# Softmax sums kept and divided out behind attention: forgetting heads on y^T, differential heads in the norm

## The chip, the core and the metric

The kernel runs on one core of one Trainium2 chip. The metric is the device time of one execution in microseconds, and lower is better. Everything is float32 at the level of the reference; TensorE works on pairs of a high and a low part.

## The reference

One decoder block on x of 1024 positions by 1024 channels. Two attention branches run side by side, each is gated, projected and merged.

```python
h = rms_norm(x, g_pre[l], NORM_EPS)
proj = jnp.einsum('bsd,dn->bsn', h, w_in[l])
qa, ka, va, fa, za, qb, kb, vb, zb, gates = jnp.split(proj, SPLIT_POINTS, axis=-1)
# forgetting heads (8 of 64 channels): softmax over causal logits plus sums of log_f
p = jax.nn.softmax(logits, axis=-1)
ya = merge_heads(p @ va) * jax.nn.silu(za)
# differential heads (4, q and k in two halves of 64, v of 128)
p = jax.nn.softmax(logits, axis=-1)
pd = p[:, :, 0] - lam * p[:, :, 1]
yb = rms_norm(pd @ vb, g_subln[l], SUBLN_EPS) * (1.0 - lam_init)
yb = merge_heads(yb) * jax.nn.silu(zb)
gate_a, gate_b = jnp.split(jax.nn.sigmoid(gates), N_BRANCHES, axis=-1)
merged = gate_a * (ya @ w_branch[l, 0]) + gate_b * (yb @ w_branch[l, 1])
x = x + rms_norm(merged @ w_out[l], g_post[l], NORM_EPS)
```

A softmax row is the exponentials divided by their sum. That sum is one number for each head and position, so it can be divided out before or after the product with v. The norm over the 128 channels of a differential head doesn't change under a factor for a position, but for its small constant.

## The kernel before

A product of two float32 matrices is made of three products of high and low parts. The high part is a cast on ScalarE, the low part the difference on VectorE or GpSimd. The order of the instructions on each engine is laid down when the kernel is built, by a scheduler that places them along a timeline of its own; buffers rotate in pools.

The stages, with their times in the profiled execution: the norm, x^T and the projections of v (0 to 113 us); attention (113 to 598); sums of x^T halves for Winograd products and the first, plain gate pass (598 to 650); seven paired gate passes d=1 to 7 (650 to 773); branch products (775 to 863); the output product and the last norm.

Attention has eight units. Units 0 to 3 are differential heads (t = 0 to 3), units 4 to 7 pairs of forgetting heads (t = 4 to 7). A unit works through groups of two blocks of 128 query positions. For each block, `s_row` (L380 to L401) makes the logits on TensorE, VectorE adds the mask or bias and takes the row's minimum (L393; the sign is turned), ScalarE takes the exponential with the row's sum in `le` (L398), and VectorE its reciprocal (L400). A forgetting head's row is scaled by it on GpSimd (L512). In a differential head the second sum's reciprocal is multiplied by minus lambda (L481), the second half scaled by that on GpSimd (L482), the first half scaled by its own on ScalarE (L484), and the two are added on GpSimd (L485). `av` (L403 to L453) turns the blocks on TensorE (L420), splits them on ScalarE and VectorE (L423, L424) and multiplies by v (L444), which gives y^T, channels by positions. y^T is stored in DRAM (`y_d`). Between groups stand, as filling for TensorE, the q and k projections of the next unit, the projections of z (stored in `z_d`), and for differential heads `sum_squares` and `subln_scales` (L357 to L361), which makes the norm's factor of each position, 4 KB a head, stored in `rs_d`. The function `rstd_of` (L108 to L110) is two GpSimd operations.

In a paired gate pass, `gates_pair` loads two weight blocks raw_0 and raw_1 (L789, from a pool with two buffers of that kind). `left_operands` makes the seven left sides of a Winograd product: raw blocks or their sums S_g (L646, GpSimd), each cast by ScalarE (L633) with the low part on VectorE, or GpSimd for raw blocks m=2 and m=4 (L634). `wino` multiplies (L682), ScalarE copies the first result (L685) and VectorE adds the others (L675) into c_g and cu_g; these get a sigmoid (L744) and are stored in `g_d` (L745). Next to that, `y_work(t, c)` (L731 to L741) finishes half of one y^T, 128x512: it loads z (L734), for t under 4 also the norm's factor over all partitions (L737) and multiplies by it (L738, VectorE), then y times z (L739, GpSimd), the sigmoid of z (L740, ScalarE) and y times that (L741, VectorE). The names yd and yf are the differential and the forgetting heads' y^T, zs and rb the loaded tiles. The forgetting heads' parts come in d=5 (t=4), d=6 (t=5) and d=7 (t=6 and 7). The tiles c_g, cu_g, zs and rb share eight buffers. Then y^T is split (L824, L825), and the branch products (L835) begin with the forgetting heads; their weights are cast on ScalarE (hi_br, L229), the low part on VectorE or GpSimd (lo_br, L233).

## Time and profile before

| what | us |
|---|---|
| median of 3 runs (lowest and highest) | 963.38 (962.74 to 963.75) |
| profiled execution, its own time | 964.18 |
| its span | 962.4 |
| TensorE busy in the span | 900.5 |
| VectorE busy | 635.3 |
| GpSimd busy | 489.6 |
| ScalarE busy | 435.9 |

A profile is one execution, taken by the hardware profiler; times are microseconds from the start of the span, unless marked ns. Engines: PE is TensorE's matmul, PEld its load of weights, DVE VectorE, ACT ScalarE, POOL GpSimd, SP the engine that issues the DMAs; a name with q behind is an engine's sequencer. PEclk is the clock granted to TensorE, 1.00 is full speed. "A <- B" in the waits means that A stood idle until B was done. The chain is the work that ended last, followed back from the last instruction to what released it. L12 is line 12 of the kernel, out<-in names the tiles.

### The profile page before, as it was taken

Reading aid. Unit: us, or ns where it says so; the run is one execution under the profiler, and the core shown is the slowest. Engines: PE = TensorE matmul, PEld = TensorE weight load, DVE = VectorE, ACT = ScalarE, POOL = GpSimd, SP = SyncE. Lnnn points to the kernel's source line nnn. Section 1 sums busy time; section 2 is a strip of 40 time slices with the busy share of each in tenths; the row PEclk is TensorE's granted clock in tenths of the full one; section 3 lists DMA queues with packets and bytes.
Section 4 is the critical chain, followed back from the end, with each engine's and each line's share of the span. In section 5 each row is a group of like instructions: output and inputs, shape, how many; then the busy total and the mean of one; then the engine's idle time right before and its main releaser. Section 6 shows DMA issues by size and latency. Waiting matters only on the chain.

```text
span 962.4 us, 13682 instructions
## 1 busy us (share of the span) xinstructions
PE 900.5 (94%) x4600; PEld 752.0 (78%) x4600; DVE 635.3 (66%) x1180; ACT 435.9 (45%) x862; POOL 489.6 (51%) x460
## 2 busy tenths in 40 slices
PE   7999989999999999999999998879999989999992
PEld 5999867777887888888888886658887768887871
DVE  7731258978768765656566477985667683559875
ACT  3421125665656674555555566243444361324331
POOL 7100035446545464344533554935566735878972
PEclk9999989999999999999999999989999999999997
DMA  9532444424334341524225231254444697210144
GB/s 315 190 110 93 144 128 112 107 77 120 97 96 137 99 144 43 150 67 130 81 88 146 85 88 56 78 179 149 143 153 134 191 357 247 67 44 1 46 151 153
DMA packets 109896, 120.17 MB, mean 125 GB/s; under 512 B 9969, under 2 KB 79601, under 8 KB 109826
## 3 DMA queue, kind: packets, MB, share of 16 engines
q1 hardware_dynamic: 109826, 119.30, 40.0%
q8 instruction: 36, 0.59, 0.3%
q14 instruction: 34, 0.28, 0.1%
HBM read 77.26 MB, written 29.43 MB: 111 GB/s over the span
## 4 chain that ended last, share of the span: by engine, by line
PE 45%; DVE 17%; POOL 13%; issue 10%; DMA 7%; ACT 6%; SPq 2%; DVEq 0%; POOLq 0%; ACTq 0%
PE pb L835 9%; PE pv L192 9%; PE pz L243 7%; PE pq L243 5%; PE pk L243 4%; POOL S_g L646 3%; PE ypf L444 3%; PE ptf L420 2%; DMA raw<-in_w_in_dram 2%; DMA swk<-rawk 2%; SPq L284 2%; DVE Pd L393 1%; POOL a_g L634 1%; PE ypd L444 1%; PE Sf L391 1%
## 5 line engine op out<-in xcount | busy, mean ns | idle before, releaser
L192 PE MATMUL pv<-wvhi,hT 128*128 128x264 f32 (+2 forms) x384 | 88.8, 323 | 0.4 <-DVE hT L178 0.4
L682 PE MATMUL x_g<-T,a_g 128*128 128x512 f32 x336 | 82.1, 399 | 6.3 <-DVE a_g L634 2.5
L243 PE MATMUL pk<-hT,hi_k 128*128 128x512 f32 x256 | 84.5, 402 | 1.7 <-ACT rawk L280 1.7
L243 PE MATMUL pz<-hT,hi_z 128*128 128x512 f32 x256 | 84.2, 399 | 0.1
L243 PE MATMUL pq<-hT,hi_q 128*128 128x512 f32 x256 | 83.4, 399 | 0.0
L682 PEld LDWEIGHTS x_g<-T,a_g 128*128 128x128 f32 x336 | 63.4, 191 | 23.5 <-DVE a_g L634 4.0
L835 PE MATMUL pb<-yT,hi_br 128*128 128x512 f32 x256 | 78.9, 390 | 1.9 <-ACT hi_br L229 1.6
L682 PE MATMUL x_o<-wo_op,a_o 128*128 128x512 f32 x336 | 77.4, 391 | 2.3 <-ACT a_o L633 1.2
L682 PEld LDWEIGHTS x_o<-wo_op,a_o 128*128 128x128 f32 x336 | 62.8, 188 | 16.9 <-ACT a_o L633 2.1
L192 PEld LDWEIGHTS pv<-wvhi,hT 128*128 128x128 f32 x384 | 64.3, 189 | 6.1 <-DVE hT L178 0.7
L682 PE MATMUL x_g<-hT,a_g 128*128 128x512 f32 x252 | 62.2, 400 | 6.1 <-DVE a_g L634 5.4
L398 ACT ACTIVATE Pd<-Pd,mxd 128x128 f32<-128x128 f32 (+7 forms) x64 | 49.5, 773 | 29.9 <-DVE mxd L393 28.1
L512 POOL TENSOR_SCALAR Pf<-Pf,lf 128x1024 f32<-128x1024 f32 (+3 forms) x64 | 47.9, 752 | 29.0 <-DVE lf L400 27.2
L424 DVE TENSOR_TENSOR plf<-ptf,phf 128x512 fp32r<-128x512 f32 (+1 forms) x80 | 50.0, 635 | 18.8 <-ACT phf L423 17.8
L192 PE MATMUL pv<-wvlo,hT 128*128 128x512 f32 (+2 forms) x192 | 61.8, 324 | 0.6 <-DVE wvlo L148 0.6
L682 PEld LDWEIGHTS x_g<-hT,a_g 128*128 128x128 f32 x252 | 48.4, 193 | 17.6 <-DVE a_g L634 5.8
L482 POOL TENSOR_SCALAR Pd<-Pd,ld 128x128 f32<-128x128 f32 (+7 forms) x32 | 25.5, 798 | 71.1 <-DVE ld L481 38.2
L508 POOL TENSOR_TENSOR cb<-cb,trim 128x128 f32<-128x128 f32 x64 | 29.5, 464 | 63.3 <-DVE mxf L393 46.7
L398 ACT ACTIVATE Pf<-Pf,mxf 128x1024 f32<-128x1024 f32 (+3 forms) x64 | 49.7, 778 | 21.4 <-DVE mxf L393 20.8
L835 PEld LDWEIGHTS pb<-yT,hi_br 128*128 128x128 f32 x256 | 47.8, 188 | 12.7 <-ACT hi_br L229 2.0
L243 PEld LDWEIGHTS pk<-hT,hi_k 128*128 128x128 f32 x256 | 48.0, 192 | 11.2 <-issue 2.1
L243 PEld LDWEIGHTS pq<-hT,hi_q 128*128 128x128 f32 x256 | 48.0, 191 | 9.1
(243 smaller groups left out, 2440.5 us busy)
## 6 DMA issues: line engine op xcount, KB each, us to landing
raw<-in_w_in_dram SPq DMA_DIRECT2D x14, 512.0 KB, 4.0
g_d<-c_g SPq DMA_DIRECT2D x21, 256.0 KB, 2.0
vb_d<-vbs SPq DMA_DIRECT2D x8, 512.0 KB, 5.9
va_d<-vas SPq DMA_DIRECT2D x8, 512.0 KB, 3.0
raw_k<-in_w_in_dram SPq DMA_DIRECT2D x8, 512.0 KB, 4.3
raw_q<-in_w_in_dram SPq DMA_DIRECT2D x8, 512.0 KB, 4.4
V<-vb_d SPq DMA_DIRECT2D x4, 1024.0 KB, 7.4
raw_z<-in_w_in_dram SPq DMA_DIRECT2D x8, 512.0 KB, 5.4
```

The source lines that it names most:

```text
L192: nc.tensor.matmul(ps[n], lhsT=hT[hp][k // 4][i // 4][:, k % 4, hs], rhs=wt[k][:, a:b], start=first, stop=(k == KT - 1 and hp == 1))
L243: nc.tensor.matmul(ps, lhsT=a[:, k, :], rhs=hT[h][k // 4][c][:, k % 4, :], start=(k == 0 and a is hi and h == 0), stop=(k == KT - 1 and a ...
L284: nc.sync.dma_start(sw[b * 32:(b + 1) * 32, :], raw[o * 32:(o + 1) * 32, :])
L398: nc.scalar.activation(pr[:, 0:n], pr[:, 0:n], AF.Exp, bias=mx[:, len(pcs) - 1:len(pcs)], scale=-1.0, accum_out=le)
L424: nc.vector.tensor_tensor(pl[:, 0:n], pt[:, 0:n], ph[:, 0:n], op=ALU.subtract)
L444: nc.tensor.matmul(o, lhsT=a, rhs=b[:, src], start=(j == 0 and n == 0), stop=(odd == 1 and jj == g and n == len(prods) - 1))
L482: nc.gpsimd.tensor_scalar(p2[:, 0:n], p2[:, 0:n], l2, 1.0, op0=ALU.mult, op1=ALU.mult)
L508: nc.gpsimd.tensor_tensor(diag, diag, trim, op=ALU.add)
L512: nc.gpsimd.tensor_scalar(p1[:, 0:n], p1[:, 0:n], l1, 1.0, op0=ALU.mult, op1=ALU.mult)
L646: eng.tensor_tensor(comb[name], x, y, op=op)
L682: nc.tensor.matmul(x[m], lhsT=a[:, ai, k, :], rhs=right[m][bi][k], start=(k == 0 and n == 0), stop=(k == 3 and n == 2))
L835: nc.tensor.matmul(ps, lhsT=a[:, kk, :], rhs=yT[g][h][:, k % 2, sl], start=(k == 0 and a is hi and h == 0), stop=(k == 3 and a is lo))
```

## The change

The sums are kept in a tile `lsum` (12 heads, 128 positions by 8 blocks), where the exponential writes them.

For forgetting heads the exponentials go into the product with v as they are. After a unit, VectorE takes the reciprocals of 128x8 a head, and `save_sums` stores them in `l_d` in DRAM, by position, one DMA a head. `y_work` loads them over 64 partitions for each of the two heads (into rb, two DMAs) and multiplies y^T by rb on VectorE, ahead of the multiplication by z.

For differential heads the first half stays unscaled, and the second is scaled by minus lambda times the first sum over the second. So y^T is larger by the first sum. The norm takes that away, if its constant is multiplied by the square of the sum: `subln_scales` loads the saved sums, GpSimd squares them, and VectorE adds them to the sum of squares.

The diff's core:

```diff
@@ -92,6 +92,9 @@
     onesr = const.tile([P, 32], F32R, name="onesr")
     nc.gpsimd.tensor_scalar(onesr, ident[:, 0:32], 0.0, 1.0, op0=ALU.mult, op1=ALU.add)
     sub_rs = const.tile([P, 4, 8], F32, name="sub_rs")
+    sub_l = const.tile([P, 4, 8], F32, name="sub_l")
+    lsum = const.tile([P, 12, 8], F32, name="lsum")
+    linv = const.tile([P, 8, 8], F32, name="linv")
 
     hT = [[[hpool.tile([P, 4, CH], F32R, tag=f"h{part}{kh}{sh}", name=f"hT{part}{kh}{sh}")
             for sh in range(2)] for kh in range(2)] for part in range(2)]
@@ -102,6 +105,7 @@
     y_d = [dram.tile([P, S], F32, name=f"y_d{t}") for t in range(8)]
     g_d = [[dram.tile([P, S], F32, name=f"g_d{d}_{b}") for b in range(2)] for d in range(KT)]
     ss_d = dram.tile([4, S], F32, name="ss_d")
+    l_d = dram.tile([12, S], F32, name="l_d")
     rs_d = dram.tile([4, S], F32, name="rs_d")
     z_d = [dram.tile([P, S], F32, name=f"z_d{t}") for t in range(8)]
 
@@ -355,9 +359,12 @@
             nc.sync.dma_start(ss_d[t:t + 1, sl], sq[0:1])
 
         def subln_scales(t):
-            rs = sub_rs[:, t]
+            rs, ls = sub_rs[:, t], sub_l[:, t]
             nc.sync.dma_start(rs, ss_d[t].rearrange("(p j) -> p j", j=8))
-            rstd_of(rs, rs, P, SUB_EPS)
+            nc.sync.dma_start(ls, l_d[8 + t].rearrange("(p j) -> p j", j=8))
+            nc.gpsimd.tensor_tensor(ls, ls, ls, op=ALU.mult)
+            nc.vector.scalar_tensor_tensor(rs, ls, P * SUB_EPS, rs, op0=ALU.mult, op1=ALU.add)
+            rstd_of(rs, rs, P, 0.0)
             nc.sync.dma_start(rs_d[t].rearrange("(p j) -> p j", j=8), rs)
 
         def pieces(i):
@@ -377,7 +384,11 @@
                 nc.sync.dma_start(f32(t[a]), f32(src[b, qs]))
             return t
 
-        def s_row(T, m, i, X, bias, boff, nm):
+        def save_sums(h, src):
+
+            nc.sync.dma_start(l_d[h].rearrange("(i p) -> p i", p=P), src)
+
+        def s_row(T, m, i, X, bias, boff, nm, le):
 
             A, B = (T["TA"], T["KA"]) if m == 0 else (T["TB"], T["KB"])
             n = (i + 1) * P
@@ -394,11 +405,9 @@
                     out=pr[:, a:b], in0=ps, in1=bias[:, boff + a:boff + b], scale=-0.125,
                     scalar=BIG if j == 0 else mx[:, j - 1:j], op0=ALU.add, op1=ALU.min,
                     accum_out=mx[:, j:j + 1])
-            le = small.tile([P, 1], F32, tag="l", name=f"l{nm}_{m}_{i}", bufs=8)
             nc.scalar.activation(pr[:, 0:n], pr[:, 0:n], AF.Exp,
                                  bias=mx[:, len(pcs) - 1:len(pcs)], scale=-1.0, accum_out=le)
-            nc.vector.reciprocal(le, le)
-            return pr, le
+            return pr
 
         def av(rows, g, vt, hoff, fox, evac, nm, final):
 
@@ -475,13 +484,17 @@
                     boff = S - (i + 1) * P
                     if "X" not in rows:
                         rows["X"] = [swapped(T, m, i // 2, f"d{u}") for m in range(2)]
-                    p1, l1 = s_row(T, 0, i, rows["X"][0], dmask, boff, f"d{u}")
-                    p2, l2 = s_row(T, 1, i, rows["X"][1], dmask, boff, f"d{u}")
+
+                    l1 = lsum[:, 8 + u, i:i + 1]
+                    l2 = small.tile([P, 1], F32, tag="l", name=f"l{u}_{i}", bufs=8)
+                    p1 = s_row(T, 0, i, rows["X"][0], dmask, boff, f"d{u}", l1)
+                    p2 = s_row(T, 1, i, rows["X"][1], dmask, boff, f"d{u}", l2)
                     n = (i + 1) * P
-                    nc.vector.tensor_tensor(l2, l2, nlam, op=ALU.mult)
+                    nc.vector.reciprocal(l2, l2)
+                    nc.vector.tensor_scalar(
+                        l2, l2, l1, nlam, op0=ALU.mult, op1=ALU.mult)
                     nc.gpsimd.tensor_scalar(
                         p2[:, 0:n], p2[:, 0:n], l2, 1.0, op0=ALU.mult, op1=ALU.mult)
-                    nc.scalar.activation(p1[:, 0:n], p1[:, 0:n], AF.Copy, scale=l1)
                     nc.gpsimd.tensor_tensor(
                         p1[:, 0:n], p1[:, 0:n], p2[:, 0:n], op=ALU.add)
                     rows[i] = p1
@@ -508,10 +521,8 @@
                     nc.gpsimd.tensor_tensor(diag, diag, trim, op=ALU.add)
                     if "X" not in rows:
                         rows["X"] = swapped(T, m, i // 2, f"f{u}")
-                    p1, l1 = s_row(T, m, i, rows["X"], cb[m], 0, f"f{u}")
-                    nc.gpsimd.tensor_scalar(
-                        p1[:, 0:n], p1[:, 0:n], l1, 1.0, op0=ALU.mult, op1=ALU.mult)
-                    rows[i] = p1
+                    h = 2 * t + m
+                    rows[i] = s_row(T, m, i, rows["X"], cb[m], 0, f"f{u}", lsum[:, h, i:i + 1])
 
                 def evac(m, g):
                     def run(yp):
@@ -611,6 +622,12 @@
                 while nf < len(fill) and nf < len(fill) * done / total:
                     fill[nf]()
                     nf += 1
+            if u < 4:
+                save_sums(8 + u, lsum[:, 8 + u])
+            else:
+                for h in (2 * u - 8, 2 * u - 7):
+                    nc.vector.reciprocal(linv[:, h], lsum[:, h])
+                    save_sums(h, linv[:, h])
         pend()
 
     bigs.close()
@@ -732,10 +749,17 @@
         ys = yz[t // 2][:, t % 2, c * CH:(c + 1) * CH]
         zs = tmp.tile([P, CH], F32, tag="t", name=f"zs{t}_{c}")
         nc.sync.dma_start(zs, z_d[(t + 4) % 8][:, c * CH:(c + 1) * CH])
+        rb = tmp.tile([P, CH], F32, tag="t", name=f"rb{t}_{c}")
         if t < 4:
-            rb = tmp.tile([P, CH], F32, tag="t", name=f"rb{t}_{c}")
             nc.sync.dma_start(rb, rs_d[t:t + 1, c * CH:(c + 1) * CH].to_broadcast([P, CH]))
             nc.vector.scalar_tensor_tensor(ys, ys, gsub, rb, op0=ALU.mult, op1=ALU.mult)
+        else:
+            for m in range(2):
+                h = 2 * t - 8 + m
+                nc.sync.dma_start(
+                    rb[64 * m:64 * m + 64],
+                    l_d[h:h + 1, c * CH:(c + 1) * CH].to_broadcast([64, CH]))
+            nc.vector.tensor_tensor(ys, ys, rb, op=ALU.mult)
         nc.gpsimd.tensor_tensor(ys, ys, zs, op=ALU.mult)
         nc.scalar.activation(zs, zs, AF.Sigmoid)
         nc.vector.tensor_tensor(ys, ys, zs, op=ALU.mult)
```

The scheduler's order moves with it, since its timeline moves. Three places follow. In the changed kernel the lines are shifted: L398 is L408, L633 and L634 are L650 and L651, L646 is L663, L675 is L692, L685 is L702, L738 to L741 are L755 and L763 to L765, L744 is L768, and the new multiplication is L762. Numbers behind a name only tell buffers apart.

First, ScalarE at the first rows of the second differential unit, where the scale L484 stood between the exponentials. Before:

```order
L398 ACTIVATE Pd_0_0_1948,ld_0_0_1954<-Pd_0_0_1948,mxd_0_0_1949 128x128
L398 ACTIVATE Pd_1_0_1957,ld_1_0_1963<-Pd_1_0_1957,mxd_1_0_1958 128x128
L398 ACTIVATE Pd_0_1_1970,ld_0_1_1976<-Pd_0_1_1970,mxd_0_1_1971 128x256
L484 ACTIVATE Pd_0_0_1948<-Pd_0_0_1948,ld_0_0_1954 128x128
L484 ACTIVATE Pd_0_1_1970<-Pd_0_1_1970,ld_0_1_1976 128x256
L423 CAST phd_3_0_1994<-ptd_3_0_1993 128x512
L292 CAST KA_1940<-rawk_0_2086 64x512
L294 CAST KB_1941<-rawk_0_2086 64x512
L423 CAST phd_3_1_2003<-ptd_3_1_2002 128x512
```

Now:

```order
L408 ACTIVATE Pd_0_0_1930,lsum<-Pd_0_0_1930,mxd_0_0_1931 128x128
L408 ACTIVATE Pd_1_0_1937,l_0_1929<-Pd_1_0_1937,mxd_1_0_1938 128x128
L408 ACTIVATE Pd_0_1_1949,lsum<-Pd_0_1_1949,mxd_0_1_1950 128x256
L296 CAST KA_1921<-rawk_0_2061 64x512
L432 CAST phd_3_0_1969<-ptd_3_0_1968 128x512
L298 CAST KB_1922<-rawk_0_2061 64x512
L432 CAST phd_3_1_1978<-ptd_3_1_1977 128x512
```

The scales are gone, the exponential writes its first sum into lsum, and the casts follow the exponentials directly.

Second, the gate pass d=5, from the last sums S_g on. GpSimd before:

```order
L646 TENSOR_TENSOR S_g_7669<-raw_0_7607,raw_1_7609 128x512
L646 TENSOR_TENSOR S_g_7711<-raw_0_7607,S_g_7631 128x512
L739 TENSOR_TENSOR yf_7439<-yf_7439,zs_0_7597 128x512
L739 TENSOR_TENSOR yd_6964<-yd_6964,zs_1_7589 128x512
L739 TENSOR_TENSOR yf_7439<-yf_7439,zs_1_7602 128x512
L634 TENSOR_TENSOR a_g_7692<-raw_0_7607,a_g_7692 128x512
L634 TENSOR_TENSOR a_g_7732<-raw_1_7609,a_g_7732 128x512
```

GpSimd now:

```order
L663 TENSOR_TENSOR S_g_7425<-raw_0_7363,raw_1_7365 128x512
L663 TENSOR_TENSOR S_g_7467<-raw_0_7363,S_g_7387 128x512
L763 TENSOR_TENSOR yd_6712<-yd_6712,zs_1_7337 128x512
L651 TENSOR_TENSOR a_g_7448<-raw_0_7363,a_g_7448 128x512
L763 TENSOR_TENSOR yf_7187<-yf_7187,zs_0_7345 128x512
L763 TENSOR_TENSOR yf_7187<-yf_7187,zs_1_7354 128x512
L651 TENSOR_TENSOR a_g_7488<-raw_1_7365,a_g_7488 128x512
```

ScalarE before, in the same pass:

```order
L633 CAST a_g_7692<-raw_0_7607 128x512
L740 ACTIVATE zs_0_7597<-zs_0_7597 128x512
L744 ACTIVATE c_g_7505<-c_g_7505 128x512
L740 ACTIVATE zs_1_7589<-zs_1_7589 128x512
L633 CAST a_g_7713<-S_g_7711 128x512
L740 ACTIVATE zs_1_7602<-zs_1_7602 128x512
L744 ACTIVATE cu_g_7487<-cu_g_7487 128x512
L685 COPY c_g_7627<-x_g_7614 128x512
L633 CAST a_g_7732<-raw_1_7609 128x512
```

ScalarE now:

```order
L650 CAST a_g_7448<-raw_0_7363 128x512
L768 ACTIVATE c_g_7253<-c_g_7253 128x512
L764 ACTIVATE zs_1_7337<-zs_1_7337 128x512
L650 CAST a_g_7469<-S_g_7467 128x512
L764 ACTIVATE zs_0_7345<-zs_0_7345 128x512
L768 ACTIVATE cu_g_7235<-cu_g_7235 128x512
L764 ACTIVATE zs_1_7354<-zs_1_7354 128x512
L702 COPY c_g_7383<-x_g_7370 128x512
L650 CAST a_g_7488<-raw_1_7365 128x512
```

On GpSimd yd now stands first, a low part next, and the two yf follow right before the last low part, that of raw_1. On ScalarE the last sigmoid of zs has moved from ahead of cu_g's sigmoid to behind it, still ahead of the copy of c_g and of the cast of raw_1. The pass d=6 has the same order.

Third, VectorE at the end of d=7. Before, up to the split of y^T (L825):

```order
L634 TENSOR_TENSOR a_g_8015<-raw_0_7941,a_g_8015 128x512
L741 TENSOR_TENSOR yf_7442<-yf_7442,zs_0_7921 128x512
L741 TENSOR_TENSOR yd_6964<-yd_6964,zs_1_7913 128x512
L675 TENSOR_TENSOR cu_g_7811<-x_g_7897,cu_g_7811 128x512
L741 TENSOR_TENSOR yf_7442<-yf_7442,zs_1_7926 128x512
L741 TENSOR_TENSOR yf_7442<-yf_7442,zs_0_7931 128x512
L634 TENSOR_TENSOR a_g_8066<-S_g_8064,a_g_8066 128x512
L741 TENSOR_TENSOR yf_7442<-yf_7442,zs_1_7936 128x512
```

Now:

```order
L762 TENSOR_TENSOR yf_7190<-yf_7190,rb_0_7687 128x512
L651 TENSOR_TENSOR a_g_7795<-raw_0_7721,a_g_7795 128x512
L765 TENSOR_TENSOR yd_6712<-yd_6712,zs_1_7677 128x512
L692 TENSOR_TENSOR cu_g_7575<-x_g_7661,cu_g_7575 128x512
L762 TENSOR_TENSOR yf_7190<-yf_7190,rb_1_7696 128x512
L765 TENSOR_TENSOR yf_7190<-yf_7190,zs_0_7685 128x512
L762 TENSOR_TENSOR yf_7190<-yf_7190,rb_0_7705 128x512
L651 TENSOR_TENSOR a_g_7846<-S_g_7844,a_g_7846 128x512
L765 TENSOR_TENSOR yf_7190<-yf_7190,zs_1_7694 128x512
L762 TENSOR_TENSOR yf_7190<-yf_7190,rb_1_7714 128x512
L765 TENSOR_TENSOR yf_7190<-yf_7190,zs_0_7703 128x512
L765 TENSOR_TENSOR yf_7190<-yf_7190,zs_1_7712 128x512
```

Four multiplications by rb have come in, the second behind cu_g, the third behind the multiplication of yf by the first zs, the fourth behind that by the second.

## The prediction

> **What bounds the kernel now.** I read the page first, then the table by stage, then the waits and the chain inside each stage. The page says that TensorE is the bound on average:
>
> ```profile
> span 962.4 us, 13682 instructions
> PE 900.5 (94%) x4600; PEld 752.0 (78%) x4600; DVE 635.3 (66%) x1180; ACT 435.9 (45%) x862; POOL 489.6 (51%) x460
> ```
>
> An average hides stages. The next view has the busy time of each engine by stage: 140–262 are the first differential heads, 262–360 the others, 360–604 the forgetting heads with their tail from 575 on, 650–765 the paired gate passes, then the branch products.
>
> ```profile
> core 0: us, PE busy (x) PEld busy (x) DVE busy (x) ACT busy (x) POOL busy (x), PEclk, DMA share, GB/s
> 140.00:262.00 122.00, 115.89 (x584) 96.59 (x582) 102.62 (x231) 72.32 (x149) 63.74 (x52) 0.96 0.40 104
> 262.00:360.00 98.00, 95.79 (x519) 80.35 (x519) 71.29 (x189) 63.40 (x131) 50.88 (x46) 1.00 0.41 118
> 360.00:575.00 215.00, 212.60 (x1218) 183.33 (x1218) 130.19 (x346) 118.48 (x254) 95.54 (x132) 1.00 0.34 98
> 575.00:604.00 29.00, 24.98 (x160) 20.57 (x159) 21.38 (x55) 18.25 (x46) 15.94 (x24) 1.00 0.21 74
> ...
> 650.00:765.00 115.00, 112.13 (x489) 90.82 (x488) 73.88 (x90) 46.94 (x82) 72.05 (x50) 1.00 0.49 154
> 765.00:863.00 98.00, 95.22 (x418) 77.83 (x417) 57.58 (x62) 31.37 (x39) 64.23 (x34) 1.00 0.54 182
> ```
>
> What attention can win is what TensorE lacks there: 122.00 − 115.89 = 6.1 us, then 2.2, 2.4 and 4.0, together 14.7 us, plus the clock of 0.96 in the first stage. In the stage of the forgetting heads TensorE is 99% busy, so whatever leaves another engine there is nearly all hidden. The waits (who waited for whom: total, times, longest) of 140–262, and below the dots two of 360–575:
>
> ```profile
> ACT Pd L484 <- DVE ld L400: 16.5, 13, 4.0
> ACT Pd L398 <- DVE mxd L393: 11.4, 10, 1.9
> POOL swq L286 <- DMA swq<-rawq: 11.3, 5, 3.3
> ```
>
> ```profile
> POOL Pf L512 <- DVE lf L400: 25.5, 25, 3.2
> ...
> POOL sub_rs L109 <- DMA sub_rs<-ss_d: 4.4, 3, 1.9
> ```
>
> Such a wait is idle time of an engine, not of the kernel. The chain that ended last says how much counted. In 140–262 the scale L484 is on it five times (first and last shown; 0.40, 1.04, 0.54, 0.40 and 0.42 us, 2.80 us in all), in 360–575 the scale L512 once:
>
> ```profile
> 147.25 0.40 ACT Pd L484
> ...
> 261.28 0.42 ACT Pd L484
> ```
>
> ```profile
> 566.29 1.14 POOL Pf L512
> ```
>
> In the gate passes the same view shows a loop. The weights of the next pass can only be loaded once the last reader of the old raw_1 is done, and that reader comes at the end of this row of hand-overs (pass d=5):
>
> ```profile
> 718.82 1.30 POOL yd L739
> ...
> 720.15 0.64 ACT zs L740
> ...
> 722.29 0.69 DVE cu_g L675
> ...
> 723.54 0.57 ACT c_g L685
> 724.11 0.53 ACT a_g L633
> ...
> 724.70 1.30 POOL a_g L634
> ...
> 726.02 4.65 DMA raw<-in_w_in_dram
> ```
>
> The loads of raw_1 that follow each other have these rows on SP (the one between them is the 726.02 above):
>
> ```profile
> 704.85 0.59 SPq L789 DMA_DIRECT2D raw<-in_w_in_dram  x1
> ...
> 746.62 0.38 SPq L789 DMA_DIRECT2D raw<-in_w_in_dram  x1
> ```
>
> A pass takes 21.2 and 20.6 us. So the passes go by this loop and not by TensorE alone, although it is 97% busy there. That is where the new multiplications stand.
>
> **What leaves.** Counts and times of the removed rows (min/median/max ns):
>
> ```profile
> L400 DVE RECIPROCAL ld<-ld x64: 144/158/167, 147.1 to 356.6; 128x1 f32<-128x1 f32 x64
> L484 ACT ACTIVATE Pd<-Pd,ld x32: 387/776/1154, 147.2 to 358.4; 128x128 f32<-128x128 f32 x4, 128x256 f32<-128x256 f32 x4, 128x384 f32<-128x384 f32 x4, 128x512 f32<-128x512 f32 x4
> L512 POOL TENSOR_SCALAR Pf<-Pf,lf x64: 372/753/1143, 359.6 to 593.7; 128x1024 f32<-128x1024 f32 x8, 128x896 f32<-128x896 f32 x8, 128x768 f32<-128x768 f32 x8, 128x640 f32<-128x640 f32 x8
> ```
>
> All 32 of L484 go (32 × 0.776 ≈ 25 us of ScalarE), all 64 of L512 (64 × 0.753 ≈ 48 us of GpSimd), half of the differential reciprocals and all 64 of the forgetting heads. ScalarE no longer stands 16.5 us behind L400 with later exps queued. But behind these waits stand others of nearly the same size (11.4 and 11.3 us above), so I credit what the chain held, 2.8, rounded to −3.0 for 140–262 (ends 0 and −6.1, the idle of TensorE). For 262–360 no L484 lies on the chain: −0.5 (0 to −2.2). For 360–575 the one piece of L512: −1.1 (0 to −2.4). For the tail, in which nothing fills TensorE, I take −0.5 of its 4.0 (0 to −2). Sum: −5.1 us.
>
> **What comes in attention.** Twelve stores of sums with 4-byte pieces, each 1024 of them, and four small loads. Nearest rows: the store of the same size in 32-byte pieces, and a transfer with 1024 packets:
>
> ```profile
> rs_d<-sub_rs SPq DMA_DIRECT2D x4, 4.0 KB, 1.7
> ...
> V<-vb_d SPq DMA_DIRECT2D x4, 1024.0 KB, 7.4
> ```
>
> Each should land between 1.7 and 7.4 us after its issue. All but the last are read tens of us later, so they cost nothing; the last ones are a rival below. In the norm's step VectorE now waits for a load and for a square on GpSimd, where GpSimd waited before (4.4 us in 3 times, 1.5 each). Behind that wait stand the next row minima (L393) and the splits (L424) for TensorE; the projections that fill TensorE hide it. Without this cover it would be four times up to 1.9, +7.6. Taken: +0.5 (0 to +7.6; no gain, since nothing is taken off VectorE here). The new reciprocals of 128x8 are 8 in place of 64 and cost nothing.
>
> **What comes in the gate passes.** Eight multiplications yf by rb on VectorE. Their shape is that of L741, and what follows is fixed by L739 and L740:
>
> ```profile
> L741 DVE TENSOR_TENSOR yf<-yf,zs x8: 677/1286/1560, 719.3 to 770.4; 128x512 f32<-128x512 f32 x8
> ...
> L739 POOL TENSOR_TENSOR yf<-yf,zs x8: 1733/1748/1754, 715.8 to 767.9; 128x512 f32<-128x512 f32 x8
> ...
> L740 ACT ACTIVATE zs<-zs x16: 629/632/637, 661.7 to 769.7; 128x512 f32<-128x512 f32 x16
> ```
>
> In d=5 and d=6 the second one stands behind the multiplication of yd on VectorE, after which cu_g began at 722.29. It ends 0.68 to 1.56 after that, at 722.97 to 723.85. Then GpSimd multiplies yf by zs (1.75: 724.7 to 725.6), then ScalarE takes the sigmoid (0.63: 725.35 to 726.2). In the new order this sigmoid stands ahead of the copy of c_g and of the cast of raw_1, where the old order had it early. The copy, at 723.54 before, starts at 725.35 to 726.2: the load of raw_1 is 1.8 to 2.7 us late, and the loop passes that on. I take the middle, 2.25, twice: +4.5 (3.6 to 5.4). The two half loads of rb that it needs stand on SP behind a store of gates; I take them as landed by then, and a late one would come on top of these ends.
>
> In d=7 there are four more multiplications, and no load is waited for. What counts is the end: the last sigmoid, then four casts of y, then the first weights of the branch:
>
> ```profile
> 765.05 0.68 DVE L675 TENSOR_TENSOR cu_g<-x_g,cu_g 128x512 f32<-128x512 f32 x1
> ```
>
> ```profile
> 769.72 0.63 ACT L740 ACTIVATE zs<-zs 128x512 f32<-128x512 f32 x1 [2.26 <-POOL yf L739]
> ```
>
> ```profile
> 775.14 1.20 PE L835 MATMUL pb<-yT,hi_br 128*128 128x512 f32 x4 [1.60 <-ACT hi_br L229]
> ```
>
> In the new order, from cu_g on: the second multiplication ends at 765.5 to 767.2; yf on GpSimd 1.75; sigmoid 0.63; L741 0.68 to 1.56; the fourth multiplication the same; yf 1.75; sigmoid 0.63: 771.7 to 775.1, where 770.35 was before, so +1.3 to +4.8. VectorE has no idle time ahead of the row of 765.05; if it has none up to the end either, four more operations of 0.68 to 1.56 are +2.7 to +6.2. Ends 1.3 and 6.2, taken in the middle: +3.75. TensorE, which already waits 1.60 for this, pays all of it.
>
> **Sum.** −5.1 + 0.5 + 4.5 + 3.75 = +3.65 us. The profiled execution took 964.18 us around its span of 962.4; with the change 967.8. Against the median 963.38 the same difference gives 967.0.
>
> **Rivals.** *Attention wins more* (faster). ScalarE without L484 takes exps earlier, VectorE, the busiest after TensorE in 140–262, loses small operations, and TensorE gets back all 6.1 us there, with 1.1, 0.5 and 1.3 behind: −9.0; the multiplications run at their short end (+3.6 + 1.3). Net −4.1: 959.3. For it: 16.5 us of waits in one place. Against: 2.8 us on the chain. It decides once attention gives over 10 us or the gate side costs under 3.
>
> *Even* (within 0.2%, 1.9 us, about what a measurement of this kernel can tell from no change). Attention −6, gates +3.6, end +2.4: 963.4.
>
> *GpSimd and VectorE in each other's way* (slower still). The row of L741 has 0.68 and 1.56 us for one and the same operation. If all eight fall on a busy GpSimd, the passes cost 5.4 and the end 6.2, with 0.5 and −5.1: +7.0, 970.4. The Trainium skill, "SBUF — State Buffer", section "SBUF: two separate sides", says that a VectorE operation with two SBUF inputs and a GpSimd operation that reads SBUF exclude each other for the whole instruction, and the second waits. The trace agrees with 1.56 against 0.68 us; by that rule alone the long ends hold, and the result would be this rival's.
>
> *The clock falls* (slower still). TensorE would stand idle 1.60 + 3.75 = 5.35 us in one piece before the branch products. Rows of the trace with 5.35 us of idle and with 2.78 us in pieces:
>
> ```profile
> 620.00:628.00 8.00, 2.65 (x9) 1.86 (x8) 8.00 (x8) 1.24 (x2) 6.17 (x5) 0.80 0.00 0
> 772.00:780.00 8.00, 5.22 (x21) 3.28 (x20) 8.00 (x8) 8.00 (x10) 3.03 (x1) 1.00 0.97 338
> ```
>
> Granted 0.80 for 8 us costs 1.6 us: 968.6. The Trainium skill, "TensorE: Matmul & The Clock Gate", section "What's actually happening", says that after an idle window of about 3.4 us the clock is halved until the array has been busy as long. Both rows agree with that.
>
> *The last sums delay the last y.* The chain ends attention with the load behind the last y store:
>
> ```profile
> 598.78 4.44 DMA y_d<-ys
> ```
>
> If the stores of sums stand in its way for the 7.4 − 1.7 = 5.7 us between the two rows, the time is 972.7. That the change does not do what it says is excluded by the order: L484 and L512 are gone from it.
>
> **Chances.** Forecast (965.3 to about 969) 0.34; exclusion 0.12, clock 0.08, sums 0.04; even 0.19; attention wins more 0.23. So faster 0.23, same 0.19, slower 0.58. The range goes from the faster rival's 959.3, cut to 959.0, to the long ends with the clock, 970.4 + 1.6 = 972.0. Alone, the slower cases span 965.3 to 972.7.
>
> **What would show it.** Right: in 140–262 the stage shrinks by about 3 us, in 360–575 hardly; the loads of raw_1 in d=5 and d=6 are issued some 23 us after the one before instead of 21.2 and 20.6; the first branch product starts some 5 us after the last gate product instead of 1.6, with ScalarE's last sigmoid late. Wrong: if those periods stay, if the idle stretch before the branch products does not grow, or if the attention stages shrink by more than 8 us together.

## The result and the profile after

The change makes the kernel slower: 1008.19 us (median of 4 runs, 1005.90 to 1011.77) against 963.38. The ratio is 1.047, with a 95% interval of 1.0442 to 1.0490. The forecast was 967.0, and the range ended at 972.0.

The page after:

```profile
span 1008.3 us, 13527 instructions
PE 913.5 (91%) x4600; PEld 761.6 (76%) x4600; DVE 617.4 (61%) x1104; ACT 416.1 (41%) x830; POOL 436.0 (43%) x400
```

The work left as counted: GpSimd has 53.6 us less than the 489.6 of before, ScalarE 19.8 less, VectorE 17.9 less. The span is 46 us longer. Of that, 32.9 us are idle time of TensorE, and 13.0 are its own time, 913.5 against 900.5 for the same 4600 products. In attention its clock was granted at 0.93 and 0.97 in rows that had 1.00 before. The stages, with their bounds moved to the same places of the work:

```profile
core 0: us, PE busy (x) PEld busy (x) DVE busy (x) ACT busy (x) POOL busy (x), PEclk, DMA share, GB/s
140.00:262.00 122.00, 113.40 (x575) 94.04 (x574) 91.41 (x211) 60.05 (x131) 61.22 (x51) 0.97 0.44 98
262.00:382.00 120.00, 106.53 (x550) 89.45 (x550) 74.64 (x182) 58.05 (x123) 52.56 (x48) 0.93 0.42 102
382.00:609.00 227.00, 214.53 (x1196) 183.35 (x1196) 123.48 (x298) 117.04 (x252) 55.89 (x82) 0.97 0.43 94
609.00:640.00 31.00, 19.06 (x136) 16.22 (x135) 17.30 (x43) 16.73 (x42) 12.45 (x15) 0.89 0.52 36
```

In the second row TensorE lacks 13.5 us where it lacked 2.2, in the third 12.5 where it lacked 2.4, in the tail 11.9 instead of 4.0. The start and the end of groups of instructions give the loss by place. The rows are the products with v of the differential and of the forgetting heads, before (L444) and after (L453), and the branch products after (first and last start behind the durations):

```profile
L444 PE MATMUL ypd<-pld,V x80: 273/279/387, 163.9 to 382.3; 128*128 128x256 f32 x64, 128*128 128x128 f32 x16
...
L444 PE MATMUL ypf<-plf,V x160: 272/281/387, 388.2 to 597.3; 128*128 128x256 f32 x128, 128*128 128x128 f32 x32
```

```profile
L453 PE MATMUL ypd<-pld,V x80: 273/280/415, 164.3 to 401.9; 128*128 128x256 f32 x64, 128*128 128x128 f32 x16
...
L453 PE MATMUL ypf<-plf,V x160: 272/282/389, 408.0 to 630.4; 128*128 128x256 f32 x128, 128*128 128x128 f32 x32
...
L859 PE MATMUL pb<-yT,hi_br x256: 389/389/796, 820.7 to 909.3; 128*128 128x512 f32 x128
```

Before, the branch products began at 775.1. So 19.6 us are lost up to the last differential product and 33.1 up to the last forgetting one. The tail loses more, and the stage behind it gives some back: at the load of raw_1 ahead of d=5 the loss is 35.9 (740.75 against 704.85), and at the first branch product 45.6. It stays so to the end.

Where from, SP's rows tell, around the store of the second differential head's sums. What stands behind a DMA on SP is issued behind it:

```profile
253.90 0.38 SPq L389 DMA_DIRECT2D l_d<-lsum  x1
...
256.77 0.39 SPq L229 DMA_DIRECT2D raw_q<-in_w_in_dram  x1
266.09 0.33 SPq L364 DMA_DIRECT2D sub_l<-l_d  x1
266.51 0.47 SPq L384 DMA_DIRECT2D X0d<-TA  x1
```

The load of the sums, which reads what the store writes, stands a few places behind it, and SP issues nothing more from 256.77 to 266.09. The swapped halves of the queries (X0d), from which TensorE makes logits, stand behind that load. The chain has these waits and the others of their kind:

```profile
253.90 12.13 DMA l_d<-lsum
...
371.95 10.19 DMA l_d<-lsum
...
445.37 7.30 DMA cb<-cum_d
...
454.04 11.23 DMA cb<-cum_d
...
625.12 12.60 DMA y_d<-ys
```

A store of 4 KB is on the chain with 12.13 and 10.19 us. Loads of the next unit's bias (cb) take 7.3 and 11.2 us near the stores of linv, and the last y, 4.44 us before, takes 12.60. On GpSimd the new square waits for the loaded sums, and the sums of the two halves of a row (L498) queue up behind it; the rows of TensorE are those of 180 to 400 us:

```profile
POOL sub_l L365 <- DMA sub_l<-l_d: 29.6, 4, 12.2
...
PEld ptd L429 <- POOL Pd L498: 15.5, 3, 8.0
PE ptd L429 <- POOL Pd L498: 14.3, 3, 7.6
```

In the gate passes, the loads of raw_1 stand at 720.31, 740.75, 764.46 and 786.52: the periods of d=5 and d=6 are 23.7 and 22.1 us, and 21.2 and 20.6 before:

```profile
740.75 0.38 SPq L813 DMA_DIRECT2D raw<-in_w_in_dram  x1
...
764.46 0.38 SPq L813 DMA_DIRECT2D raw<-in_w_in_dram  x1
...
786.52 0.38 SPq L813 DMA_DIRECT2D raw<-in_w_in_dram  x1
```

And TensorE waits 6.49 us for the branch's first weights, where it waited 1.60:

```profile
820.66 2.93 PE L859 MATMUL pb<-yT,hi_br 128*128 128x512 f32 x6 [6.49 <-ACT hi_br L233]
```

### The profile page after: what moved, and what is told of

Same layout as the page of the kernel before. It is cut to its first block, busy times and chain, and to the rows that moved or that the text cites. A ratio compares the mean times of both kernels' runs of the same rounds, so it can differ in the third digit from the quotient of the medians.

```text
span 1008.3 us, 13527 instructions
## 1 busy us (share of the span) xinstructions
PE 913.5 (91%) x4600; PEld 761.6 (76%) x4600; DVE 617.4 (61%) x1104; ACT 416.1 (41%) x830; POOL 436.0 (43%) x400
## 4 chain that ended last, share of the span: by engine, by line
PE 37%; DVE 16%; DMA 16%; issue 12%; POOL 11%; ACT 5%; SPq 2%; DVEq 0%; POOLq 0%; ACTq 0%
PE pb L859 8%; PE pv L196 8%; PE pz L247 6%; PE pq L247 3%; PE pk L247 2%; DMA cb<-cum_d 2%; DMA l_d<-lsum 2%; PE ypf L453 2%; POOL S_g L663 2%; PE ptf L429 2%; DMA raw<-in_w_in_dram 2%; DMA swk<-rawk 2%; DMA y_d<-ys 1%; DMA rb<-l_d 1%; DVE Pd L404 1%
## 5 line engine op out<-in xcount | busy, mean ns | idle before, releaser
L699 PE MATMUL x_g<-T,a_g 128*128 128x512 f32 x336 | 85.3, 409 | 9.8 <-ACT a_g L650 5.6
L247 PE MATMUL pk<-hT,hi_k 128*128 128x512 f32 x256 | 87.0, 412 | 1.9 <-ACT rawk L284 1.8
L408 ACT ACTIVATE Pd<-Pd,mxd 128x128 f32<-128x128 f32 (+7 forms) x64 | 49.6, 776 | 85.6 <-DVE mxd L404 82.6
L408 ACT ACTIVATE Pf<-Pf,mxf 128x1024 f32<-128x1024 f32 (+3 forms) x64 | 49.8, 778 | 38.3 <-DVE mxf L404 38.0
L699 PE MATMUL x_g<-hT,a_g 128*128 128x512 f32 x252 | 59.3, 389 | 0.0
L247 PEld LDWEIGHTS pz<-hT,hi_z 128*128 128x128 f32 x256 | 47.9, 190 | 14.2 <-issue 4.7
L247 PEld LDWEIGHTS pk<-hT,hi_k 128*128 128x128 f32 x256 | 49.5, 198 | 11.9 <-issue 2.2
L247 PE MATMUL pk<-hT,lo_k 128*128 128x512 f32 x128 | 52.6, 411 | 2.0 <-DVE lo_k L237 2.0
```

Source lines behind the costliest of these rows:

```text
L247: nc.tensor.matmul(ps, lhsT=a[:, k, :], rhs=hT[h][k // 4][c][:, k % 4, :], start=(k == 0 and a is hi and h == 0), stop=(k == KT - 1 and a ...
L408: nc.scalar.activation(pr[:, 0:n], pr[:, 0:n], AF.Exp, bias=mx[:, len(pcs) - 1:len(pcs)], scale=-1.0, accum_out=le)
L699: nc.tensor.matmul(x[m], lhsT=a[:, ai, k, :], rhs=right[m][bi][k], start=(k == 0 and n == 0), stop=(k == 3 and n == 2))
```

## The experiments

In the runs below the kernel before, on the same chips, was at 964.6 to 966.0 in the median of each set and spread from 960.4 to 968.8, so the ratios to it count and not the microseconds.

Theory 1 was that the stores in 4-byte pieces make the loss of attention. The rival was that the new order of attention, with unscaled rows and a new wait of VectorE, is slower by itself.

### 32-byte pieces

```diff
-            nc.sync.dma_start(l_d[h].rearrange("(i p) -> p i", p=P), src)
+            nc.sync.dma_start(l_d[h].rearrange("(p j) -> p j", j=8), src)
```

> The changed kernel with the sums stored in 32-byte pieces (eight numbers of a partition side by side) instead of 4-byte pieces; the reader behind takes them in that order, so positions are mixed up in the scale factors. Everything else is as in the change. Theory 1 (the twelve stores in 4-byte pieces hold up SP, GpSimd and the queues behind them): such a store lands in about 2 us as rs_d does, attention loses its 33 us and the end of attention its 8, 965 to 975 in all. Rival (the new order in attention, with unscaled rows and a new wait of VectorE in the norm's step, is slower by itself): 995 to 1010.

Measured: 971.01 us (968.76 to 971.18), ratio 1.0050 (1.0030 to 1.0071). The time of the change falls by 37 us with the shape of twelve small stores. The trace has attention's end, the last product of the forgetting heads, at 593.3, ahead of the 597.3 of before, and the loads of sums follow their stores by 1.4 to 3.3 us:

```profile
189.99 0.34 SPq L389 DMA_DIRECT2D l_d<-lsum  x1
191.43 0.33 SPq L364 DMA_DIRECT2D sub_l<-l_d  x1
251.32 0.33 SPq L389 DMA_DIRECT2D l_d<-lsum  x1
254.66 0.53 SPq L364 DMA_DIRECT2D sub_l<-l_d  x1
```

The rival is out: the same order of attention with harmless stores ends 4 us earlier than before, not later:

```profile
L453 PE MATMUL ypf<-plf,V x160: 272/282/387, 382.9 to 593.3; 128*128 128x256 f32 x128, 128*128 128x128 f32 x32
```

What is left over the kernel before lies behind attention.

### The load of the sums later

```diff
+            nc.sync.dma_start(ls, ss_d[t].rearrange("(p j) -> p j", j=8))
             nc.sync.dma_start(ls, l_d[8 + t].rearrange("(p j) -> p j", j=8))
```

> The changed kernel with the 4-byte stores kept, but the sums for the norm are loaded only when the sum of squares is there (another small load into the same tile goes ahead of it), so that load no longer stands right behind the store on SP. Theory 1: what SP waits for behind a store (8.8 to 12.2 us, four times) and GpSimd's waits for the loaded sums go, most of the 17 us that the differential units lost; transfers issued behind a store still land late: 985 to 997. Rival (new order in attention): 1003 to 1012.

Measured: 992.78 us (991.89 to 993.44), ratio 1.0283 (1.0259 to 1.0307): 15 us less than the change. GpSimd's wait for the sums falls to a third, that for the bias stays as in the change (44.8 us there, 12.1 before):

```profile
POOL cb L522 <- DMA cb<-cum_d: 44.1, 5, 12.9
...
POOL sub_l L366 <- DMA sub_l<-l_d: 9.5, 4, 5.9
```

So the load that stands right behind a store on SP is a part of the loss, by the ratios 1.8% of the 4.2% that the 4-byte stores cost.

### The stores alone, added to the kernel before

```diff
...
+            for h in ((8 + u,) if u < 4 else (2 * u - 8, 2 * u - 7)):
+                nc.sync.dma_start(l_d[h].rearrange("(i p) -> p i", p=P), lsum[:, h])
         pend()
```

The dots stand for the tile `lsum`, in which the sums and their reciprocals are now made, and for `l_d`.

> The kernel before with the twelve 4-byte stores added alone, at the places of the change; nothing reads them, and the results are as before. Theory 1: what is issued behind a store lands late, without any wait on the store itself: 970 to 985. Rival: nobody waits for the stores, 963 to 965.

Measured: 990.99 us (985.55 to 992.13), ratio 1.0246 (1.0205 to 1.0287). That is above what theory 1 expected, and the rival is out: nothing reads these stores, and still the chain is full of late transfers near them.

```profile
191.45 14.11 DMA l_d<-lsum
...
503.35 15.21 DMA cb<-cum_d
...
612.80 14.31 DMA y_d<-ys
```

The last y_d takes 14.31 us instead of 4.44, and a bias 15.21. The first row is a store itself, though nothing reads it. The kernel's DMAs take eight semaphores (the counters that tell of a landing) in turn, and SP doesn't issue a DMA before the one eight before it has landed. The first load of swk is the eighth behind this store, and SP stood 2.9 us for it until the store had landed at 205.55. How much of the loss goes by such waits, and how much by transfers that land late, no run here parts. These 2.5% are about what the later load left of the 4.2%.

### The same stores in 8-byte pieces

Against the kernel with the stores alone:

```diff
-                nc.sync.dma_start(l_d[h].rearrange("(i p) -> p i", p=P), lsum[:, h])
+                nc.sync.dma_start(l_d[h].rearrange("(i p j) -> p i j", p=P, j=2), lsum[:, h].rearrange("p (i j) -> p i j", j=2))
```

> The kernel before with the twelve stores of sums added alone, as in the run of that kind, but in 512 pieces of 8 bytes each instead of 1024 of 4. Nothing reads them. Theory 1, with the price by the piece: half of the 25 us, 972 to 979. Rival, a price by the store: 985 to 992.

Measured: 966.34 us (964.01 to 968.80), ratio 1.0014 (0.9997 to 1.0032). Neither expectation holds: half of the pieces cost not half but about a seventeenth, and the interval reaches down to no cost at all. These stores landed 4.1 to 5.8 us after their issue. The queue's lines of the pages, of the kernel before, of 4-byte and of 8-byte stores, have the packets, the megabytes and the time of the packets as a share of 16 engines' span:

```profile
q1 hardware_dynamic: 109826, 119.30, 40.0%
```

```profile
q1 hardware_dynamic: 122306, 119.35, 45.7%
```

```profile
q1 hardware_dynamic: 116162, 119.35, 41.2%
```

With the spans 962.4, 990.4 and 963.8 the packets took 6159, 7242 and 6353 us of engine time. The 4-byte stores add 12,480 packets and 1083 us, the 8-byte stores 6336 packets and 194 us. For each added packet that is 87 and 31 ns. So it is not the number of pieces alone: a 4-byte piece costs nearly three times an 8-byte one. These are prices, not durations of the small packets, since the packets of other transfers on the queue may have become slower. The next run parts the two.

### The 4-byte stores, issued by ScalarE

Against the kernel with the stores alone:

```diff
-                nc.sync.dma_start(l_d[h].rearrange("(i p) -> p i", p=P), lsum[:, h])
+                nc.scalar.dma_start(l_d[h].rearrange("(i p) -> p i", p=P), lsum[:, h])
```

> The kernel before with the twelve 4-byte stores added alone, issued by ScalarE and not by SP. Nothing reads them. Theory (the pieces fill the DMA engines that all transfers share, whoever issues them): as from SP, 984 to 993. Rival (only what is issued behind them from the same engine is late): 963 to 970.

Measured: 986.76 us (986.22 to 987.18), ratio 1.0228 (1.0199 to 1.0256). The transfers of SP are late though the stores are not in its queue (q10 is ScalarE's):

```profile
608.15 16.68 DMA y_d<-ys
```

```profile
q1 hardware_dynamic: 109826, 119.30, 44.9%
q10 hardware_dynamic: 12480, 0.05, 1.2%
```

SP's queue has the same 109,826 packets as before, and with the span of 985.3 they took 7078 us in place of 6159. The stores' own 12,480 took 189 us, 15 ns each. So five sixths of the added time are other transfers' packets that became slower. The eight semaphores are shared too, and SP stood 6.0 us for the first store of ScalarE. But that is not all: the six transfers that SP issued from 190.20 to 198.61, around that store at 190.76 and ahead of this wait, landed 10.0 to 14.9 us after their issue, where the same ones took 2.0 to 4.3 before. What is shared, then, lies behind the queues as well.

### The sums turned on TensorE first

```diff
-            nc.sync.dma_start(l_d[h].rearrange("(i p) -> p i", p=P), src)
+            nt = 8 * (2 if h < 8 else 1)
+            ps = pj.tile([P, CH], F32, tag="pj", name=f"lt{h}")[0:nt, 0:P]
+            nc.tensor.transpose(ps, src, ident)
+            sb = stg.tile([16, P], F32, tag="lt", name=f"ls{h}", bufs=1)[0:nt]
+            nc.scalar.copy(sb, ps)
+            nc.sync.dma_start(l_d[h:h + nt // 8].rearrange("h (i p) -> (h i) p", p=P), sb)
...
```

The two forgetting heads of a unit now share one store.

> The change with the sums turned on TensorE (eight small transposes) and copied by ScalarE, so that the store has 8 or 16 pieces of 512 bytes. Complete computation. Theory 1: attention is as fast as before or faster by up to 5, the gate passes keep their loss of about 10: 965 to 974. Rival (new order): 995 to 1010.

Measured: 980.66 us (977.43 to 982.82), ratio 1.0155 (1.0124 to 1.0187). This is the whole change in a usable form, 28 us under it, but slower than before and 7 above the end of what was expected. Its trace has the last forgetting product at 600.7 (593.3 with 32-byte stores) and the first branch product at 792.0 (781.4). What makes the difference was not found.

### The gate passes: multiplications, loads, neither

Theory 2 came from the trace of the change: VectorE's new multiplications took 0.8 us in the median, and VectorE stood idle for rb before each of the eight. The kernel with 32-byte stores is the base, and three kernels take parts of it away.

```profile
L762 DVE TENSOR_TENSOR yf<-yf,rb x8: 692/813/1491, 756.2 to 812.8; 128x512 f32<-128x512 f32 x8
its engine sat idle before it (us, times) until:
  DMA rb<-l_d: 8.8, 8
```

Multiplications without loads:

```diff
-            for m in range(2):
-                h = 2 * t - 8 + m
-                nc.sync.dma_start(
-                    rb[64 * m:64 * m + 64],
-                    l_d[h:h + 1, c * CH:(c + 1) * CH].to_broadcast([64, CH]))
-            nc.vector.tensor_tensor(ys, ys, rb, op=ALU.mult)
+            nc.vector.tensor_tensor(ys, ys, zs, op=ALU.mult)
...
```

> The kernel with 32-byte stores, in which the eight multiplications of yf by rb become multiplications by zs, which is loaded anyway; the sixteen half loads of rb are left out (the result is scaled by z once more and not by the sums). Theory 2 (the gate passes lose their time to late loads of rb, not to the multiplications): the 10.7 us between the start of d=5 and the branch products go but for 0 to 3: 960 to 964. Rival 2 (the multiplications and their place in the order, as forecast, 8 us): 968 to 971.

Measured: 968.43 us (966.37 to 970.44), ratio 1.0038 (1.0022 to 1.0053). Rival 2 has it.

Loads without multiplications:

```diff
-            nc.vector.tensor_tensor(ys, ys, rb, op=ALU.mult)
```

> The kernel with 32-byte stores, in which the half loads of rb stay and the multiplications by them are left out. With multiplications alone the stretch from d=5 to the branch products lost 6.1 us and with both 10.7. Theory (the loads cost only where a multiplication waits for them): as without both, 958 to 962. Rival (the loads by themselves, by their buffers, their place on SP and their traffic, delay what stands behind): 963 to 967.

Measured: 964.99 us (959.91 to 966.21), ratio 0.9998 (0.9980 to 1.0015). That is the rival's time. Against the kernel with neither, below, the loads that nobody waits for still seem to cost something, though the two intervals overlap.

Neither:

```diff
-        rb = tmp.tile([P, CH], F32, tag="t", name=f"rb{t}_{c}")
         if t < 4:
+            rb = tmp.tile([P, CH], F32, tag="t", name=f"rb{t}_{c}")
...
-        else:
-            for m in range(2):
...
-            nc.vector.tensor_tensor(ys, ys, rb, op=ALU.mult)
```

> The kernel with 32-byte stores, in which the forgetting heads' y is not scaled at all: neither the sixteen half loads of rb nor the eight multiplications (the sums are stored and not used). Theory: attention keeps its gain of some 4 us and the gate passes lose nothing, 958 to 962. Rival (the passes are slower by another move of the order, or the gain is given back on the way): 963 to 968.

Measured: 961.16 us (959.47 to 966.01), ratio 0.9968 (0.9950 to 0.9987). Without the step in the gate passes, the gain of attention reaches the end of the kernel.

The loads on another engine's queue:

```diff
-                nc.sync.dma_start(
+                nc.scalar.dma_start(
                     rb[64 * m:64 * m + 64],
```

> The kernel with 32-byte stores, in which the sixteen half loads of rb are issued by ScalarE and not by SP, so that they don't stand behind stores of gates there. Theory 2 with the queue of SP as the cause: 961 to 967. If the loads are late for another reason (their buffers come free late, or they land slowly), or if issuing them holds up ScalarE: 969 to 974.

Measured: 970.71 us (967.63 to 974.13), ratio 1.0066 (1.0043 to 1.0089): no gain over the base. In its trace the loads do come earlier: VectorE waits 5.4 us for rb in 4 times, and 9.1 in 8 in the base, and the first branch product waits 2.41 us in place of 5.90. But it starts at 782.8, and at 781.4 in the base. So their place on SP did make them late, and what takes the gain away was not found.

Counted from the kernel with neither (0.9968), the loads alone add 0.30% (2.9 us of 963.4), the multiplications alone 0.70% (6.7 us), both 0.82% (7.9 us). Each of these ratios has an interval of about 0.2% either way, and within that the sum of the parts and the whole agree. Theory 2 falls as the only cause: the multiplications cost the larger part without the loads. The first branch product shows the stretch in the traces. Its start and its wait with both, with multiplications alone, with loads alone, and with neither:

```profile
781.43 2.93 PE L859 MATMUL pb<-yT,hi_br 128*128 128x512 f32 x6 [5.90 <-ACT hi_br L233]
```

```profile
777.22 2.93 PE L854 MATMUL pb<-yT,hi_br 128*128 128x512 f32 x6 [2.26 <-ACT hi_br L233]
```

```profile
773.17 1.21 PE L858 MATMUL pb<-yT,hi_br 128*128 128x512 f32 x4 [1.30 <-ACT hi_br L233]
```

```profile
771.15 1.21 PE L852 MATMUL pb<-yT,hi_br 128*128 128x512 f32 x4 [1.56 <-ACT hi_br L233]
```

Loads alone don't lengthen this wait; multiplications that stand idle for their loads do. From the last forgetting product to this one the traces have 178.1 us with neither, 178.8 with loads alone, 183.5 with multiplications alone and 188.1 with both. So in the traces some 4 us come only where both are there; the ratios are too coarse to show it.

### Only the differential part

```diff
-                    rows[i] = s_row(T, m, i, rows["X"], cb[m], 0, f"f{u}", lsum[:, h, i:i + 1])
+                    l1 = lsum[:, h, i:i + 1]
+                    p1 = s_row(T, m, i, rows["X"], cb[m], 0, f"f{u}", l1)
+                    nc.vector.reciprocal(l1, l1)
+                    nc.gpsimd.tensor_scalar(
+                        p1[:, 0:n], p1[:, 0:n], l1, 1.0, op0=ALU.mult, op1=ALU.mult)
+                    rows[i] = p1
```

This is on top of the kernel that turns the sums; the stores of the forgetting heads' sums and the step in `y_work` are gone.

> Only the differential part of the change, with the sums turned on TensorE and stored in 512-byte pieces; the forgetting heads scale their rows as before. Complete computation. Theory 1: the differential units keep the gain that they showed with harmless stores (1 to 3 us), and neither the last y nor the gate passes lose: 959 to 963. Rival (that gain is given back in the forgetting heads, where TensorE has no idle time to give): 963 to 966.

Measured: 965.93 us (962.41 to 968.89), ratio 1.0013 (0.9996 to 1.0030). It is the one complete form that does not lose, and it does not win. Its last differential product is at 383.1 (382.3 before, 376.8 with 32-byte stores): with the turned sums the differential units have no gain to give.

### The differential part without any transfer of sums

```diff
-            ps = pj.tile([P, CH], F32, tag="pj", name=f"ssq{t}_{c}")[0:32]
-            nc.tensor.matmul(ps, lhsT=onesr, rhs=hi, start=True, stop=False)
-            nc.tensor.matmul(ps, lhsT=onesr, rhs=lo, start=False, stop=True)
+            ps = pj.tile([P, CH], F32, tag="pj", name=f"ssq{t}_{c}")[:, 0:P]
+            for b in range(4):
+                bs = slice(b * P, (b + 1) * P)
+                o = ps[:, 32 * b:32 * b + 32]
+                nc.tensor.matmul(o, lhsT=hi[:, bs], rhs=onesr, start=True, stop=False)
+                nc.tensor.matmul(o, lhsT=lo[:, bs], rhs=onesr, start=False, stop=True)
...
+            ps = pj.tile([P, CH], F32, tag="pj", name=f"rt{t}")[0:8, 0:P]
+            nc.tensor.transpose(ps, rs, ident)
```

> Only the differential part of the change, without any store or load of the sums: the sum of squares is made on TensorE in columns (positions over partitions, as the softmax sums lie), the factor is finished there, turned once on TensorE and stored in 512-byte pieces. Forgetting heads as before. Complete computation. Theory (the gain of the differential units was real and was lost only to the way of the sums): 959 to 963, below the kernel before by more than its interval. Rival (TensorE's 64 small products and four transposes, or another move of the order, take it back): 963 to 967.

Measured: 978.15 us (975.41 to 980.03), ratio 1.0125 (1.0103 to 1.0146). The last differential product comes at 373.0, 9.3 us earlier than before, and the last forgetting product at 609.9, 12.6 later. TensorE's work stands in another order there, so the first number by itself shows no gain. What the forgetting units lose their time to was not found.

## Why the prediction was wrong

**The step that failed** is the sentence on the stores: "All but the last are read tens of us later, so they cost nothing". It failed three times over. The sums of the differential heads were not read tens of microseconds later: the load stood a few places behind its store on SP, and the order of the instructions, which was to be had before, shows it. The store was bounded at 7.4 us by a transfer of 1024 larger packets, and it stood on the chain with 10 to 12. And a transfer that nobody reads still delays others: 2.5% for the stores alone. Together 4.2% or 40 us, nearly all of the difference between 967 and 1008 (change against 32-byte stores: ratios 1.0466 and 1.0050). Why pieces of 4 bytes are so dear stays open. Without these stores' price the sum was near: 1.0050 is 968.2 on the scale of the 963.4.

**The new wait in the norm's step** was put on VectorE and at +0.5 us, with an end of 7.6 if nothing hides it. It came on GpSimd, ahead of VectorE, with 29.6 us in four times, since the square stands in GpSimd's order soon after the store. TensorE's transposes waited some 15 us for rows of GpSimd (14.3 and 15.5 in the rows of its products and of its weight loads), and the sums of these rows stand behind the square. The kernel with the later load puts it and SP's wait together at 1.8%.

**Attention's gain** was taken as −5.1, with +0.5 for the norm. With harmless stores and no step in the gate passes the kernel is at 0.9968, −3.1 us, and the last forgetting product is 4.2 us earlier than before (593.1 against 597.3). The main place was right too: the last differential product comes 5.7 us earlier (376.6 against 382.3), where 3.5 was forecast. The forgetting units, where TensorE was 99% busy, give nothing for 48 us taken off GpSimd: 216.5 us in place of 215.0, where 1.6 less was forecast.

**The gate passes** were taken as +4.5 and +3.75. By the ratios, step and loads together cost 7.9. In the change's trace d=5 and d=6 are 2.5 and 1.5 us longer, 4.0 in place of 4.5. The end of d=7 was undersized: from the last load of raw_1 to the first branch product the trace has 5.6 us more (746.62 to 775.14 before, 786.52 to 820.66 after), since to the row of hand-overs come waits for rb, 8.8 us on VectorE in the three passes. I had taken these loads as landed, with the remark that a late one comes on top; it did. The end's lower bound was also misread: cu_g itself ends at 765.05 + 0.68, so the second multiplication can't end before 766.4, the bound is +2.2 and the middle 4.2.

**The rivals.** "The last sums delay the last y" is true with 12.60 in place of 4.44 us, 8.2 more, where 5.7 was allowed for. It was weighed at 0.04 and for the last store alone, while other transfers were late near stores all through attention. "The clock falls" came, but cost nothing at its place: behind the 6.49 us of waiting the granted clock is 0.68 from 819 to 827 us (1.00 from 773 to 781 before), and the first branch products take up to 796 ns, 389 in the median. The low part that comes next is waited for in both kernels, and the branch products take 88.8 us from the first to the last, 88.7 before. The rival looked in one place only. In attention the clock was lower too (0.93 and 0.97), and most of the 13.0 us that TensorE's own time grew by lie there; that the new waits made it fall is likely, and no run shows it. "In each other's way" is open: the multiplications took 0.69 to 1.49 us, so both prices occur.

## What to carry to other kernels

Price a small DMA by the size of its pieces, not by its bytes, and look for the row with the smallest pieces before bounding it; if the trace has none of that size, the end of the range is open, and a layout that makes 4-byte pieces is a rival by itself. Read in the order of instructions what stands behind a store on its queue, above all a load of the same data, and which in-order engine takes that load first. Count how many DMAs may be under way: with eight semaphores in turn, as here, one slow store stops the eighth DMA behind it. An operation moved out of a stage where TensorE is full wins nothing there, and costs where it goes if that place is a loop.

## What the runs showed of the hardware

A store of 4 KB from 128 partitions in 1024 pieces of 4 bytes took 10 to 14 us on the chain; in 512 pieces of 8 bytes it landed after 4.1 to 5.8 us; in 32-byte pieces its reader was issued 1.4 to 3.3 us after it. For each added packet the queues lost 87 ns at 4 bytes and 31 ns at 8 bytes. At 4 bytes most of that was not the small packets' own time (15 ns each on ScalarE's queue) but that of others: SP's unchanged packets took 7078 us in place of 6159. The Trainium skill, "DMA: Bandwidth & Descriptors", section "Specifications", says that transfers under 512 bytes are done by reading, changing and writing back. Both sizes lie under that, so this rule alone doesn't tell why 4 bytes cost so much more than 8; no run here shows the cause. The loss was the same within the intervals whether SP or ScalarE issued the stores (2.5% and 2.3%).
